# Gate and up of the feed-forward layers with the weights stationary, from the third slab on

## The chip, the cores and the metric

One core of a Trainium2 chip runs the whole program. The metric is the device time of one execution in microseconds, the median of three runs.

## The reference

The input is a sequence of 256 tokens of 1024 channels, float32. Four layers follow one another. Each has a token mixer (short convolution, pooling, differential attention, convolution) and a feed-forward layer, and each of the eight sub-layers stands between two norms. What the change touches is the feed-forward part:

```python
def _rms(x, g):
    y = xf * lax.rsqrt(jnp.mean(xf * xf, axis=-1, keepdims=True) + EPS)
    return (y * g.astype(jnp.float32)).astype(x.dtype)

def _swiglu(xn, w_gate, w_up, w_down):
    return (jax.nn.silu(xn @ w_gate) * (xn @ w_up)) @ w_down

        f = _swiglu(_rms(x, g[2]), ffn_w_gate[i], ffn_w_up[i], ffn_w_down[i])
        x = x + _rms(f, g[3])
```

The inner width of the feed-forward layer is 2816.

## The kernel before

**Precision.** Every matmul of a weight runs three times in the float32r format: a weight `raw` is split into `hi` (a cast on ScalarE, ACT) and `lo` (raw minus hi, on VectorE, DVE), an activation in the same way into `xh` and `xl` (or `hh` and `hl`, `zh` and `zl`), and hi with xh, lo with xh and hi with xl are added up in one PSUM bank.

**Tiling.** The 256 tokens are two tiles `t` of 128. The inner width is cut into NS = 11 slabs of 256 channels; a slab's weights are 256 columns of gate beside 256 columns of up. `proj` (line 263) makes one bank for one token tile and one slab: over eight pieces k of the 1024 input channels, xh or xl of the tile is the stationary operand (128x128) and 512 weight columns move, 24 matmuls. `evac` (475) takes the bank off: silu of the gate half with the token's rstd as scale on ACT, and on DVE the product with the up half and rstd, which gives `h`, tokens on the partitions. `flush` (483) turns h around with two transposes on TensorE (PE) and splits the result into hh (ACT) and hl (DVE), channels on the partitions. `down` (277) then has 128 columns of hh or hl stationary and 512 columns of the down weights moving, 12 matmuls for each token tile and slab, into four banks `acc` that stay open over the whole layer.

**Stages of a layer.** `start` (413) makes slabs 0 and 1 of token tile 0 while the norm before is still at work on tile 1. Then tile 1 of slabs 0 and 1 follows (513), and from slab 2 on (519) each turn of the loop makes both token tiles of slab s and then the down blocks of slab s-2 for both. The h of a bank is transposed after the next bank (`flush(1)`). `finish` (427) has the down blocks of the last three slabs, first all of tile 0 and then all of tile 1, with the norm (`boundary`, 336) of tile 0 beside tile 1's.

**What sets the order.** Every instruction is pinned to the program's order on its engine. `Weights` prepares the weights ahead: `pump(k)` (148) casts and subtracts up to k halves of a weight tile where fewer than NP = 12 halves are ahead of their release, and a subtraction that frees a raw tile lets the next load go on SP's queue. The places of the pump calls are therefore the places of this work in the queues of ACT and DVE. `boundary` squares and sums the sub-layer's output on ACT, multiplies it by the gain and the constant RS_C on DVE (`post`), computes the reciprocal root in seven small DVE operations and adds the result to x.

**PSUM.** Four banks acc, two banks mm (taken in turn by proj), two banks tr (transposes).

Of the kernel before, what the change touches and what calls it, by code (L numbers as in the profile page):

```python
# [9 lines left out]
F32 = mybir.dt.float32  # L10
# [143 lines left out]
class Kernel:  # L154
    def __init__(self, ctx, tc, x, w, gains, taps, pscale, lam, subg, rel, onehot, band, gcol, out):
        self.tc, self.nc = tc, tc.nc
        nc = self.nc
        self.V, self.A, self.T = Pinned(tc, nc.vector), Pinned(tc, nc.scalar), Pinned(tc, nc.tensor)
        self.G, self.SP = Pinned(tc, nc.gpsimd), Pinned(tc, nc.sync)
        self.w, self.gains, self.taps, self.out = w, gains, taps, out  # L160
        self.pscale, self.lamv, self.subg, self.rel = pscale, lam, subg, rel
        self.onehot, self.band = onehot, band
        pool = lambda name, bufs=1, **k: ctx.enter_context(tc.tile_pool(name=name, bufs=bufs, **k))
        self.c = pool("c")
        self.wraw = pool("wraw", NR)
        self.wsp = pool("wsp", NP)
        self.gp = pool("gp", 1)
        self.st = pool("st", 12)
        ps = bass.MemoryType.PSUM
        self.ps_acc = pool("ps_acc", 4, space=ps)  # L170
        self.ps_mm = pool("ps_mm", 2, space=ps)
        self.ps_tr = pool("ps_tr", 2, space=ps)
        self.dram = pool("dram", 1, space=bass.MemoryType.DRAM)
        self.wi = 0
        self.W = Weights(self, w.shape[0])
        self.x = self.c.tile([P, 2, D], F32, name="x")
        xv = x.rearrange("(t p) d -> p t d", p=P)
        self.gc = self.c.tile([P, 2, 8], F32, name="gc")
        self.A.dma_start(out=self.gc, in_=gcol)
        self.gc, self.gcp = self.gc[:, 0, :], self.gc[:, 1, :]  # L180
        xload = lambda t, h: self.SP.dma_start(
            out=self.x[:, t, h * 512 : (h + 1) * 512], in_=xv[:, t, h * 512 : (h + 1) * 512]
        )
        xload(0, 0)
        self.W.load()
        xload(1, 0)
        xload(0, 1)
        self.W.load()
        xload(1, 1)
        self.ident = self.c.tile([P, P], F32, name="ident")  # L190
        make_identity(nc, self.ident)
        self.xh = [self.c.tile([P, 8, P], F32R, name=f"xh{t}") for t in range(2)]
        self.xl = [self.c.tile([P, 8, P], F32R, name=f"xl{t}") for t in range(2)]
        self.r2 = [self.c.tile([P, 1], F32, name=f"rstd{t}") for t in range(2)]
        self.xg, self.s2 = [None, None], [None, None]

# [66 lines left out]
    def proj(self, t, slab, bank, k0=0, k1=8):  # L263

        T = self.T
        for k in range(k0, k1):
# [7 lines left out]
            if k % 2:  # L274
                self.W.used(i, c)

    def down(self, t, wid, zh, zl, accs, first, last, n_outer=False):

        T = self.T
        order = []  # L280
        for c in range(2):
            hi, lo = self.W.get(wid, c)
            order += [(c, zh, hi, 0), (c, zh, hi, 1), (c, zh, lo, 0), (c, zh, lo, 1), (c, zl, hi, 0), (c, zl, hi, 1)]
        if n_outer:
            order.sort(key=lambda o: o[3])
        left = [6, 6]
        for c, z, wt, n in order:
            left[n] -= 1
            T.matmul(
                accs[n],  # L290
                z[c],
                wt[:, n * 512 : (n + 1) * 512],
                start=first and left[n] == 5,
                stop=last and left[n] == 0,
            )
        for c in range(2):
            self.W.used(wid, c)
# [35 lines left out]
        else:  # L333
            self.A.activation(self.junk(), x, AF.Square, scale=1.0 / 32, accum_out=o)

    def boundary(self, t, m, g_post, g_pre, nxt, rstd=None, fill=()):


        V, A, W = self.V, self.A, self.W
        fill = [*fill, 0, 0, 0, 0]  # L340
        s = self.stat()
        mg = self.gp.tile([P, D], F32, tag="mg", name="mg")
# [1 line left out]
        H = [slice(0, 512), slice(512, 1024)]  # L344

        def post(h):
            V.scalar_tensor_tensor(mg[:, H[h]], m[h], RS_C, g_post[:, H[h]], op0=ALU.mult, op1=ALU.mult)

        def add(sl):
            V.scalar_tensor_tensor(x[:, sl], mg[:, sl], y, x[:, sl], op0=ALU.mult, op1=ALU.add)  # L350
# [3 lines left out]
                V.tensor_tensor(mg[:, H[h]], x[:, H[h]], g_pre[:, H[h]], op=ALU.mult)  # L354

        for h in range(2):
            A.activation(self.junk(), m[h], AF.Square, scale=1.0 / 32, accum_out=s[:, h : h + 1])
        W.sub(fill[0])
        post(0)
        W.sub(fill[1])  # L360
# [63 lines left out]
        self.x_rstd(1)  # L424


    def finish(self, outs, g_post, g_pre, nxt, zs):


        W = self.W  # L430
# [12 lines left out]
                W.pump(2)  # L443
        if nxt == "pool":
            tile(1, 0)
            self.boundary(0, accs[0], g_post, g_pre, nxt, None, (0, 0, 1, 1))
            for i in range(1, n):
                tile(1, i)
            self.boundary(1, accs[1], g_post, g_pre, nxt, None, (0, 0, 1, 1))
            return  # L450
        self.boundary(0, accs[0], g_post, g_pre, nxt)
        for i in range(n):
            if i == 2 and nxt == "x":
                self.x_transposed(0)
# [2 lines left out]
                self.x_transposed(0)  # L457
            if i == n - 3 and nxt == "x":
                W.pump(2)
        self.boundary(1, accs[1], g_post, g_pre, nxt, 0 if nxt == "x" else None)  # L460

    def ffn(self, pool, g_post, g_pre, nxt, tables=None):
        V, A, W = self.V, self.A, self.W
# [11 lines left out]
        def evac(t, s, bank):  # L475
            sg = pool.tile([P, 256], F32, tag="sg", name="sg", bufs=2)
            A.activation(sg, bank[:, 0:256], AF.Silu, scale=self.r2[t])
            h = pool.tile([P, 256], F32, tag="h", name="h", bufs=2)
            V.scalar_tensor_tensor(h, bank[:, 256:512], self.r2[t], sg, op0=ALU.mult, op1=ALU.mult)
            hs[t, s] = h  # L480
            pend.append((t, s))

        def flush(keep=0):
            while len(pend) > keep:
                t, s = pend.pop(0)
                if s not in hT:
                    hT[s] = (
                        pool.tile([P, 2, S], F32R, tag="hh", name="hh", bufs=4),
                        pool.tile([P, 2, S], F32R, tag="hl", name="hl", bufs=4),
                    )  # L490
                h, b = hs.pop((t, s)), self.tr()
                self.transposes(b, [h[:, 0:P], h[:, P : 2 * P]])
                sl = slice(t * P, (t + 1) * P)
                self.split(
                    b[:, 0:256].rearrange("p (c n) -> p c n", c=2), hT[s][0][:, :, sl], hT[s][1][:, :, sl]
                )
# [13 lines left out]
        if tables:  # L510
            next(tables, None)
        accs = [[self.acc(), self.acc()] for _ in range(2)]
        for s in range(2):
            b = self.mm()
            self.proj(1, slabs[s], b)
            evac(1, s, b)
            flush(1)
            self.pump()
        for s in range(2, NS):
            for t in range(2):  # L520
                b = self.mm()
                self.proj(t, slabs[s], b)
                evac(t, s, b)
                flush(1)
                self.pump()
            if tables:
                next(tables, None)
            if s < NS - 1:
# [4 lines left out]
        zs = []  # L533
        for s in range(NS - 3, NS):
            zh, zl = zpair(s)
            zs.append((dw[s], zh, zl, False, flush if s == NS - 2 else None))

        self.finish(accs, g_post, g_pre, nxt, zs)

    def conv(self, pool, layer, g_post, g_pre, nxt, cold=False):  # L540
        V, A, W = self.V, self.A, self.W
# [532 lines left out]
```

## Time and profile before

| | us |
|---|---|
| median of three runs | 1100.31 (1099.93 to 1101.47) |
| the profiled execution, its own time | 1100.8 |
| its span, first to last instruction | 1098.8 |

The page of the profile gives busy times of each engine, the span in 40 slices, the chain of work that ended last and the costliest groups of instructions. PE is the row of matmuls and PEld the row of weight loads, which run beside them. A matmul's duration contains its latency, and successive matmuls overlap, so what one costs in a stream is read from the distance between starts and not from its duration. In the names of a group the tile that is written stands ahead of the arrow, the moving and the stationary operand behind it.

### The profile page before, as it was taken

What the parts mean: (1) busy time and instruction counts of PE and PEld (TensorE: products, weight loads), DVE (VectorE), ACT (ScalarE), POOL (GpSimd) and SP (SyncE); (2) the same over time, 40 slices, a digit from 0 to 9 for tenths busy, and PEclk for the clock granted to TensorE, in tenths of its full rate; (3) what the DMA queues carried; (4) which work ended last, traced back from release to release, by engine and by line L of the source; (5) the groups of instructions that cost most, each with busy time, mean ns of one, the idle gap of its engine ahead of it and who ended that gap; (6) DMA issues with size and microseconds to landing.
All of it is one profiled execution on the core that took longest, in us unless ns stands there. A gap on an engine that the chain in (4) does not pass through costs nothing.

```text
span 1098.8 us, 12977 instructions
## 1 busy us (share of the span) xinstructions
PE 1085.5 (99%) x4990; PEld 885.8 (81%) x4990; DVE 696.2 (63%) x1171; ACT 529.9 (48%) x855; POOL 18.9 (2%) x40
## 2 busy tenths in 40 slices
PE   8999999999999999999999999999999999999997
PEld 6887888888888878888888788888888878888885
DVE  7877764555888464556786874545578677645543
ACT  6555553443556344445575563444445455534421
POOL 0000000000010001000000000000000000000000
PEclk9999999999999999999999999999999999999999
DMA  7864565545336556543544465545536544555421
GB/s 269 283 233 173 211 223 215 194 154 191 146 140 243 196 189 244 192 164 143 199 147 154 153 235 196 208 165 191 175 136 237 189 183 171 214 197 203 154 77 39
DMA packets 31486, 203.98 MB, mean 186 GB/s; under 512 B 3820, under 2 KB 4364, under 8 KB 8512
## 3 DMA queue, kind: packets, MB, share of 16 engines
q1 hardware_dynamic: 27648, 191.38, 47.7%
q0 software_dynamic: 3344, 11.24, 3.0%
q8 instruction: 39, 0.64, 0.2%
q10 hardware_dynamic: 432, 0.53, 0.1%
q14 instruction: 23, 0.19, 0.0%
HBM read 202.08 MB, written 2.11 MB: 186 GB/s over the span
## 4 chain that ended last, share of the span: by engine, by line
PE 94%; DVE 4%; ACT 1%; DMA 1%; issue 1%; SPq 0%; DVEq 0%; ACTq 0%
PE mm L48 62%; PE acc L48 28%; PE tr L48 4%; DVE st L48 1%; DVE lo L48 1%; DVE x L48 1%; DMA x<-in_x 1%; DVE mg L48 1%; ACT junk L48 0%; ACT xh L48 0%; DVE xl L48 0%; ACT hi L48 0%; SPq L48 0%; DVE ol L48 0%; DVE rstd L48 0%
## 5 line engine op out<-in xcount | busy, mean ns | idle before, releaser
L48 DVE TENSOR_TENSOR lo<-raw,hi 128x1024 fp32r<-128x1024 f32 (+1 forms) x374 | 426.1, 1187 | 57.7 <-ACT hi L48 56.8
L48 PE MATMUL mm<-hi,xh 128*128 128x512 f32 x976 | 390.8, 400 | 1.1 <-ACT hi L48 0.9
L48 PE MATMUL mm<-hi,xl 128*128 128x512 f32 x976 | 383.6, 393 | 0.2
L48 PE MATMUL mm<-lo,xh 128*128 128x512 f32 x976 | 382.6, 392 | 0.2 <-DVE lo L48 0.2
L48 ACT CAST hi<-raw 128x1024 fp32r<-128x1024 f32 (+1 forms) x374 | 361.6, 1028 | 12.9 <-DMA raw<-in_w 5.3
L48 PEld LDWEIGHTS mm<-hi,xl 128*128 128x128 f32 x976 | 183.3, 188 | 42.6 <-DVE xl L48 2.7
L48 PEld LDWEIGHTS mm<-hi,xh 128*128 128x128 f32 x976 | 183.5, 188 | 38.5 <-ACT hi L48 1.1
L48 PEld LDWEIGHTS mm<-lo,xh 128*128 128x128 f32 x976 | 183.7, 188 | 38.1 <-DVE lo L48 0.5
L48 ACT ACTIVATE sg<-mm,rstd 128x256 f32<-128x256 f32 x88 | 41.8, 475 | 356.6 <-PE mm L48 356.4
L48 DVE SCALAR_TENSOR_TENSOR h<-mm,rstd,sg 128x256 f32<-128x256 f32 x88 | 42.6, 484 | 263.7 <-ACT sg L48 263.7
L48 PE MATMUL acc<-hi,hh 128*128 128x512 f32 x352 | 116.9, 406 | 0.0
L48 PE MATMUL acc<-hi,hl 128*128 128x512 f32 x352 | 113.2, 395 | 0.0
L48 PE MATMUL acc<-lo,hh 128*128 128x512 f32 x352 | 112.7, 394 | 0.0
L48 PEld LDWEIGHTS acc<-lo,hh 128*128 128x128 f32 x352 | 66.2, 188 | 15.8
L48 PEld LDWEIGHTS acc<-hi,hl 128*128 128x128 f32 x352 | 66.2, 188 | 15.5
L48 PEld LDWEIGHTS acc<-hi,hh 128*128 128x128 f32 x352 | 63.3, 189 | 13.0 <-issue 0.9
L48 ACT ACTIVATE junk<-x 128x512 bf16<-128x512 f32 x30 | 18.9, 632 | 50.7 <-DVE x L48 50.7
L48 DVE TENSOR_TENSOR hl<-tr,hh 128x256 fp32r<-128x256 f32 x88 | 36.5, 415 | 2.3 <-ACT hh L48 2.3
L48 ACT ACTIVATE junk<-acc 128x512 bf16<-128x512 f32 x32 | 19.1, 598 | 32.9 <-PE acc L48 32.4
L48 PEld LDWEIGHTS tr<-ident,h 128*128 128x128 f32 x176 | 24.5, 139 | 11.7
L48 PE MATMUL tr<-ident,h 128*128 128x128 f32 x176 | 33.5, 272 | 0.0
L48 ACT CAST hh<-tr 128x256 fp32r<-128x256 f32 x88 | 32.2, 366 | 2.5 <-PE tr L48 2.5
(147 smaller groups left out, 666.7 us busy)
## 6 DMA issues: line engine op xcount, KB each, us to landing
raw<-in_w SPq DMA_DIRECT2D x179, 1024.0 KB, 4.8
gpost<-in_gains POOLq DMA_DIRECT2D x8, 512.0 KB, 4.1
gpre<-in_gains POOLq DMA_DIRECT2D x6, 512.0 KB, 5.7
raw<-in_w SPq DMA_DIRECT2D x3, 512.0 KB, 7.4
x<-in_x SPq DMA_DIRECT2D x4, 256.0 KB, 6.5
bandf<-in_band POOLq DMA_DIRECT2D x4, 256.0 KB, 4.8
skew<-scr POOLq DMA_DIRECT2D x4, 256.0 KB, 5.9
bias<-skew POOLq DMA_DIRECT2D x4, 192.0 KB, 5.5
```

The lines of the kernel that those rows point to most:

```text
L48: r = f(*a, **k)
```

## The change

Slabs 0 and 1 stay as they are, but for the rstd factor of the up half. From slab 2 on, the weights are the stationary operand: `proj_t` takes 128 columns of gate and the same 128 of up (index j, two of them in a slab) and moves both token tiles at once, 256 columns, as two pieces of 128 that lie apart in the joined tiles xhs and xls. A bank holds gate in one half and up in the other, channels on the partitions and tokens along the row. It takes 48 matmuls of 256 columns, and a slab has two such banks, as before. `evac_t` multiplies the gate half by `rows` (rstd of each token along the row, the same on every partition) on DVE, applies silu on ACT, multiplies by the up half on DVE, and writes hh and hl directly; there is no h to be transposed. One weight preparation stands between hh and hl, two behind.

The rstd factor of the up half is left out in all slabs. Down is linear, so the whole output of a layer lacks a factor per token; `boundary` puts it back with per-token scales `cols` (rstd/32 for the squares, RS_C times rstd for `post`). `rows` is made once a layer by two transposes of a tile whose columns all hold rstd.

```diff
+        self.xhs, self.xls = (self.c.tile([P, 2, 8, P], F32R, name=f"x{n}") for n in "hl")
+        self.xh, self.xl = ([a[:, t] for t in range(2)] for a in (self.xhs, self.xls))
+        self.ones = self.c.tile([P, P], F32, name="ones")
+        self.G.memset(self.ones, 1.0)
...
+    def proj_t(self, j, slab, bank):
+        T = self.T
+        for k in range(8):
+            i, c = slab[k // 4], k % 4 // 2
+            hi, lo = self.W.get(i, c)
+            xh, xl = self.xhs[:, :, k, :], self.xls[:, :, k, :]
+            for q in range(2):
+                o = (k % 2) * 512 + q * 256 + j * P
+                sl = slice(o, o + P)
+                b = bank[:, q * S : (q + 1) * S].rearrange("p (t n) -> p t n", t=2)
+                T.matmul(b, hi[:, sl], xh, start=k + q == 0, stop=False)
+                T.matmul(b, hi[:, sl], xl, start=False, stop=False)
+                T.matmul(b, lo[:, sl], xh, start=False, stop=k + q == 8)
+            if k % 2:
+                self.W.used(i, c)
...
-    def boundary(self, t, m, g_post, g_pre, nxt, rstd=None, fill=()):
+    def boundary(self, t, m, g_post, g_pre, nxt, rstd=None, fill=(), scale=None):
+        s32, sc = scale or (1.0 / 32, RS_C)
...
-            V.scalar_tensor_tensor(mg[:, H[h]], m[h], RS_C, g_post[:, H[h]], op0=ALU.mult, op1=ALU.mult)
+            V.scalar_tensor_tensor(mg[:, H[h]], m[h], sc, g_post[:, H[h]], op0=ALU.mult, op1=ALU.mult)
...
-            A.activation(self.junk(), m[h], AF.Square, scale=1.0 / 32, accum_out=s[:, h : h + 1])
+            A.activation(self.junk(), m[h], AF.Square, scale=s32, accum_out=s[:, h : h + 1])
...
-            V.scalar_tensor_tensor(h, bank[:, 256:512], self.r2[t], sg, op0=ALU.mult, op1=ALU.mult)
+            V.tensor_tensor(h, bank[:, 256:512], sg, op=ALU.mult)
...
+        def evac_t(s, j, bank):
+            sg = pool.tile([P, S], F32, tag="sg", name="sg", bufs=2)
+            V.tensor_tensor(sg, bank[:, 0:S], rows, op=ALU.mult)
+            A.activation(sg, sg, AF.Silu)
+            h = pool.tile([P, S], F32, tag="h", name="h", bufs=2)
+            V.tensor_tensor(h, bank[:, S : 2 * S], sg, op=ALU.mult)
+            new(s)
+            hh, hl = (a[:, j, :] for a in hT[s])
+            A.copy(hh, h)
+            W.pump(1)
+            V.tensor_tensor(hl, h, hh.bitcast(F32), op=ALU.subtract)
...
+        for t in range(2):
+            V.tensor_scalar(cols[:, t, 0:1], self.r2[t], 1.0 / 32, None, op0=ALU.mult)
+            V.tensor_scalar(cols[:, t, 1:2], self.r2[t], RS_C, None, op0=ALU.mult)
+            A.activation(rb[:, t, :], self.ones, AF.Copy, scale=self.r2[t])
         for s in range(2):
             b = self.mm()
             self.proj(1, slabs[s], b)
             evac(1, s, b)
+            if s == 0:
+                b = self.tr()
+                self.transposes(b, [rb[:, t, :] for t in range(2)])
+                A.copy(rows, b[:, 0:S])
             flush(1)
             self.pump()
         for s in range(2, NS):
-            for t in range(2):
+            for j in range(2):
                 b = self.mm()
-                self.proj(t, slabs[s], b)
-                evac(t, s, b)
-                flush(1)
-                self.pump()
+                self.proj_t(j, slabs[s], b)
+                evac_t(s, j, b)
+                flush()
+                W.pump(2)
...
-            zs.append((dw[s], zh, zl, False, flush if s == NS - 2 else None))
+            zs.append((dw[s], zh, zl, False, None))
+        scales = [(cols[:, t, 0:1], cols[:, t, 1:2]) for t in range(2)]
```

## Rows read from the trace of the kernel before

**Rows 1.** The page: span, busy time and share of each engine, granted clock in tenths.

```profile
span 1098.8 us, 12977 instructions
PE 1085.5 (99%) x4990; PEld 885.8 (81%) x4990; DVE 696.2 (63%) x1171; ACT 529.9 (48%) x855; POOL 18.9 (2%) x40
PEclk9999999999999999999999999999999999999999
```

**Rows 2.** The page: the chain that ended last, by engine.

```profile
PE 94%; DVE 4%; ACT 1%; DMA 1%; issue 1%; SPq 0%; DVEq 0%; ACTq 0%
```

**Rows 3.** Waits of PE: us in total, times, longest us.

```profile
PE acc L48 <- DVE lo L48: 1.5, 1, 1.5
...
PE tr L48 <- DVE mg L48: 0.2, 1, 0.2
```

**Rows 4.** The chain in order of time, one slab: start, us, what.

```profile
157.28 5.58 PE acc L48 x24
162.86 5.50 PE mm L48 x24
168.36 0.22 PE tr L48 x2
168.58 5.51 PE mm L48 x24
...
174.31 5.58 PE acc L48 x24
```

**Rows 5.** Groups by line: count, busy us, mean ns, idle before.

```profile
L48 PE MATMUL tr<-ident,h 128*128 128x128 f32 x176 | 33.5, 272 | 0.0
L48 PEld LDWEIGHTS mm<-hi,xh 128*128 128x128 f32 x976 | 183.5, 188 | 38.5 <-ACT hi L48 1.1
```

**Rows 6.** PE's instructions in order of time, pool mixer: start us, duration us.

```profile
294.05 0.40 PE L48 MATMUL mm<-bandh,xh 128*128 128x256 f32 x2
...
295.93 0.40 PE L48 MATMUL tr<-bandh,xl 128*128 128x256 f32 x2
...
303.43 0.39 PE L48 MATMUL mm<-bandh,xl 128*128 128x256 f32 x2
...
304.79 0.39 PE L48 MATMUL tr<-bandh,xl 128*128 128x256 f32 x2
305.02 0.28 PE L48 MATMUL acc<-hi,ph 128*128 128x256 f32 x1
...
310.59 0.28 PE L48 MATMUL acc<-hi,pl 128*128 128x256 f32 x1
```

**Rows 7.** Busy us by stretch: us, PE, PEld, DVE, ACT, POOL, clock, DMA share, GB/s.

```profile
162.90:168.30 5.40, 5.40 (x25) 4.37 (x24) 2.29 (x3) 0.20 (x1) 0.54 (x1) 1.00 0.98 388
305.10:310.50 5.40, 5.40 (x48) 5.40 (x47) 4.73 (x14) 3.54 (x9) 0.00 (x0) 1.00 0.15 61
```

**Rows 8.** Groups by line: evacuation of a bank and weight preparation.

```profile
L48 DVE TENSOR_TENSOR lo<-raw,hi 128x1024 fp32r<-128x1024 f32 x350 | 410.5, 1221 | 57.0 <-ACT hi L48 56.1
L48 DVE SCALAR_TENSOR_TENSOR h<-mm,rstd,sg 128x256 f32<-128x256 f32 x88 | 42.6, 484 | 263.7 <-ACT sg L48 263.7
L48 DVE TENSOR_TENSOR hl<-tr,hh 128x256 fp32r<-128x256 f32 x88 | 36.5, 415 | 2.3 <-ACT hh L48 2.3
...
L48 ACT CAST hi<-raw 128x1024 fp32r<-128x1024 f32 x350 | 347.9, 1055 | 11.6 <-DMA raw<-in_w 4.7 <-issue 3.5 <-DVE raw L48 2.2
L48 ACT ACTIVATE sg<-mm,rstd 128x256 f32<-128x256 f32 x88 | 41.8, 475 | 356.6 <-PE mm L48 356.4
L48 ACT CAST hh<-tr 128x256 fp32r<-128x256 f32 x88 | 32.2, 366 | 2.5 <-PE tr L48 2.5
```

**Rows 9.** DVE in order of time, end of the third feed-forward layer.

```profile
791.22 4.63 DVE L48 TENSOR_TENSOR lo<-raw,hi 128x1024 fp32r<-128x1024 f32 x4 [0.39 <-ACT hi L48]
```

**Rows 10.** Groups by line: DVE, 512 wide, with a scalar operand and with a constant.

```profile
L48 DVE SCALAR_TENSOR_TENSOR x<-mg,st,x 128x512 f32<-128x512 f32 x30 | 22.5, 751 | 0.9
L48 DVE SCALAR_TENSOR_TENSOR mg<-acc,gpost 128x512 f32<-128x512 f32 x32 | 21.9, 685 | 16.2 <-ACT junk L48 16.2
```

More of the change, by code (lines that the diff above doesn't have):

```diff
@@ L191, in __init__ @@
         make_identity(nc, self.ident)
-        self.xh = [self.c.tile([P, 8, P], F32R, name=f"xh{t}") for t in range(2)]
-        self.xl = [self.c.tile([P, 8, P], F32R, name=f"xl{t}") for t in range(2)]
+        self.xhs, self.xls = (self.c.tile([P, 2, 8, P], F32R, name=f"x{n}") for n in "hl")
+        self.xh, self.xl = ([a[:, t] for t in range(2)] for a in (self.xhs, self.xls))
+        self.ones = self.c.tile([P, P], F32, name="ones")
+        self.G.memset(self.ones, 1.0)
         self.r2 = [self.c.tile([P, 1], F32, name=f"rstd{t}") for t in range(2)]
@@ L424, in start, with finish @@
         self.x_rstd(1)
-    def finish(self, outs, g_post, g_pre, nxt, zs):
+    def finish(self, outs, g_post, g_pre, nxt, zs, scales=(None, None)):
         W = self.W
@@ L445, in finish @@
             tile(1, 0)
-            self.boundary(0, accs[0], g_post, g_pre, nxt, None, (0, 0, 1, 1))
+            self.boundary(0, accs[0], g_post, g_pre, nxt, None, (0, 0, 1, 1), scales[0])
             for i in range(1, n):
                 tile(1, i)
-            self.boundary(1, accs[1], g_post, g_pre, nxt, None, (0, 0, 1, 1))
+            self.boundary(1, accs[1], g_post, g_pre, nxt, None, (0, 0, 1, 1), scales[1])
             return
-        self.boundary(0, accs[0], g_post, g_pre, nxt)
+        self.boundary(0, accs[0], g_post, g_pre, nxt, scale=scales[0])
         for i in range(n):
@@ L459, in finish @@
                 W.pump(2)
-        self.boundary(1, accs[1], g_post, g_pre, nxt, 0 if nxt == "x" else None)
+        self.boundary(1, accs[1], g_post, g_pre, nxt, 0 if nxt == "x" else None, scale=scales[1])
     def ffn(self, pool, g_post, g_pre, nxt, tables=None):
@@ L478, in evac, with new @@
             h = pool.tile([P, 256], F32, tag="h", name="h", bufs=2)
-            V.scalar_tensor_tensor(h, bank[:, 256:512], self.r2[t], sg, op0=ALU.mult, op1=ALU.mult)
+            V.tensor_tensor(h, bank[:, 256:512], sg, op=ALU.mult)
             hs[t, s] = h
             pend.append((t, s))
+        def new(s):
+            if s not in hT:
+                hT[s] = (
+                    pool.tile([P, 2, S], F32R, tag="hh", name="hh", bufs=4),
+                    pool.tile([P, 2, S], F32R, tag="hl", name="hl", bufs=4),
+                )
+        def evac_t(s, j, bank):
[9 more added lines that the diff above has]
+            V.tensor_tensor(hl, h, hh.bitcast(F32), op=ALU.subtract)
         def flush(keep=0):
@@ L485, in flush @@
                 t, s = pend.pop(0)
[L486 to L490, printed above, removed]
+                new(s)
                 h, b = hs.pop((t, s)), self.tr()
@@ L512, in ffn @@
         accs = [[self.acc(), self.acc()] for _ in range(2)]
+        rows, cols = pool.tile([P, S], F32, name="rows"), pool.tile([P, 2, 2], F32, name="cols")
+        rb = pool.tile([P, 2, P], F32, name="rb")
+        for t in range(2):
+            V.tensor_scalar(cols[:, t, 0:1], self.r2[t], 1.0 / 32, None, op0=ALU.mult)
+            V.tensor_scalar(cols[:, t, 1:2], self.r2[t], RS_C, None, op0=ALU.mult)
+            A.activation(rb[:, t, :], self.ones, AF.Copy, scale=self.r2[t])
         for s in range(2):
@@ L535, in ffn @@
             zh, zl = zpair(s)
[L536 to L538 removed]
+            zs.append((dw[s], zh, zl, False, None))
+        scales = [(cols[:, t, 0:1], cols[:, t, 1:2]) for t in range(2)]
+        self.finish(accs, g_post, g_pre, nxt, zs, scales)
     def conv(self, pool, layer, g_post, g_pre, nxt, cold=False):
```

## The prediction

> **What bounds the kernel now.** I read the page from the top. The busy line [rows 1] shows TensorE (PE) busy for 1085.5 of 1098.8 us, and the clock row stands at 9 in every slice, so the clock is at its upper level throughout and the change has no cold stretch to save. The chain of work that ended last lies 94% on PE [rows 2], and the seven waits that PE has in the whole run, from 1.5 down to 0.2 us each, add up to 4.7 us [rows 3]. So whatever leaves PE's instruction stream leaves the time, and whatever enters it is paid in full. VectorE (DVE) and ScalarE (ACT) are busy for 63% and 48% [rows 1].
>
> The chain in order of time [rows 4] gives one slab of a feed-forward layer: 24 matmuls of token tile 0, two transposes, 24 matmuls of token tile 1, two transposes, 24 matmuls of the down projection. That is 5.50 + 0.22 + 5.51 + 0.22 + 5.58 = 17.03 us, and the next slab begins exactly there (174.31 - 157.28), so there is no gap in it. One matmul of 128x512 thus steps on in 5.50/24 = 229.2 ns in gate and up, and in 5.58/24 = 232.5 ns in down. One transpose is 0.11 us.
>
> **The change, part by part.**
>
> *Transposes removed.* Slabs 2 to 10 of four layers are 36 slabs, each with two pairs of transposes on the chain: 36 x 0.44 = 15.8 us. The trace has 176 of them [rows 5]; 144 go, 32 stay (slabs 0 and 1). Nothing hides them today: PE goes from the last matmul of a bank to the transposes and back.
>
> *Matmuls reshaped.* The columns that are streamed stay the same, 24 x 512 per bank then and 48 x 256 now, but there are twice as many matmuls. Each one loads its stationary operand even when it equals the one before: the counts of matmuls and of loads are the same, 4990 [rows 1], although gate and up use xh twice in a row. So the loads double as well, and everything hangs on the step of a 256-wide matmul, c. A slab's gate and up cost 5.50 + 5.51 + 0.44 = 11.45 us before, and 96 c after; break-even of this part is c = 119.3 ns.
>
> The trace shows 256-wide matmuls of the same type in the pool mixer alone [rows 6]. Three stretches give three steps. The second stage there runs 48 in a row, hi and lo moving, from 305.02 to 310.59: 47 steps of 118.5 ns. The band stage of token tile 0 goes from 294.05 to 295.93 with 16 steps, 117.5 ns. That of token tile 1 goes from 303.43 to 304.79 with 12 steps, 113.3 ns. The first of these is the nearest in length and in its accumulating on one region of a bank several times in a row, but its operands differ. The other anchor is the same operands at twice the width: half of 229.2 ns is 114.6 ns, and this is what c would be if a step were columns alone. I take c = 117 ns, in between and nearer to the longer stretches, and keep 113.3 and 118.5 as the ends that rows show. No row has a moving operand in two pieces, which the new one is (128 columns of either token tile, 4 KB apart); that could add something, and I see no reason for it to gain. So the cost of a slab goes from 11.45 to 96 x 0.117 = 11.23 us, a gain of 0.22 us, and over 36 slabs 7.9 us.
>
> At 256 columns the weight-load row of PE is full: 5.40 of 5.40 us with 256-wide matmuls, 4.37 of 5.40 with 512-wide ones [rows 7]. One load starts with every matmul in either. By the Trainium skill (TensorE: Matmul & The Clock Gate, Back-to-back issue gap) the spacing of a stream is set by the load and the matmul together, and narrow matmuls pay for it: about 81 ns at 128 columns where the columns alone give 56. An estimate by the Trainium skill's figures there, the same 25 ns for every load on top of the 109 ns that it gives for 256 columns, makes 134 ns here and a time near 1152 us; the 48 steps of 118.5 ns do not bear that out. Against it stands the Trainium skill (same title, Step-by-step: what each phase is for, step 1): loading the next weights takes no read bandwidth from the running matmul. By that one c is the half of the wide step; the stretch of 118.5 speaks against it, that of 113.3 for it. Both come back as rivals.
>
> *Added on PE:* two transposes a layer, of the rstd rows: 8 x 0.11 = 0.9 us. They stand after the first bank of token tile 1, 5.5 us after rb was asked for, so PE does not wait for them.
>
> *The evacuation.* Before, ACT (silu, 475 ns) and DVE (product, 484 ns) read the bank, then PE, ACT (366) and DVE (415) made hh and hl [rows 8]. After, DVE multiplies by the rows (nearest row: 415), ACT does silu (475), DVE the product (415), ACT hh (366), DVE hl (415). DVE thus gets 3 x 415 - 484 - 415 = 0.35 us more per bank, 0.7 us per slab of 16.8; it is busy for 63%, so this is cover and no cost. The bank is free about 1.5 us after its last matmul, and PE needs that buffer again only after the other bank of the pair, 5.6 us or more later. The down projection of a slab runs two iterations later, so it does not wait either. If that cover were gone, the 1.4 us of product and silu would show once per bank.
>
> *The moved pump.* One weight preparation (a cast of 1055 ns on ACT, a subtraction of 1221 on DVE) now stands between hh and hl, and hl is queued behind it. Someone waits for hl soon only at the end of a layer: the last slab's second half feeds the third down block. From the bank's end: 415 + 475 + 415 + 366 + 1055 + 1221 + 415 = 4.4 us, and with 0.05 us at each hand-over some 4.7. The first two down blocks cover 24 x 232.5 ns = 5.6 us, and the third, ordered by output half, reads that hl with its sixth matmul, at 6.7 us. I count nothing. In the layer read for this, four such subtractions stood in a row on DVE at that point, 4.63 us [rows 9]; if two of them came ahead of hl in place of one, hl would be 1.2 us later, still before 6.7. SP's weight loads keep their order; POOL gets one small memset, behind the identity that PE waits for at the start and ahead of nothing that is due then.
>
> *Up's scale in the norm.* The product on DVE loses its scalar operand; the post-norm product gets one in place of a constant. A 512-wide operation with such an operand takes 751 ns, one with a constant 685 [rows 10]: 66 ns, twice per boundary. Where PE's next work covers a boundary it costs nothing; it lies open at the end of the program and ahead of the pool mixer, where nothing follows that could cover it. Some 0.2 us, an estimate of three such pieces. The squares and the four small products for cols cost nothing that shows: they run while a bank of 5.5 us is filled.
>
> *Sum:* -7.9 + 0.9 + 0.2 = -6.8 us. The profiled execution took 1100.8 us (span 1098.8 and 2.0 around it), 0.5 over the median of 1100.31. I subtract from the median: **1093.5 us**.
>
> **The rivals.**
>
> *The step is columns alone.* Then c is 113.3 to 114.6 ns, a slab costs 10.88 to 11.00 us, the gain is 0.57 to 0.45 us a slab, 20.6 to 16.2 in all, and with the 1.1 us added the time is 1080.8 to 1085.2. For it: the band stretch of token tile 1, and the steady 229.2 of the same operands. Against it: the longest stretch.
>
> *The loads eat the gain.* With c = 118.5 a slab costs 11.38, the gain is 2.7 us, less 1.1 added: 1098.7, no change that can be told. For it: the longest and steadiest stretch. Against it: its operands lie elsewhere, and two of three stretches are below.
>
> *The two-piece moving operand costs (slower).* Two matmuls of 118.5 take 237.0 where one of 229.2 carries the same columns: a break between two matmuls costs 7.8 ns. If a break inside the operand costs the same, c = 126.3, a slab 12.12 us, 0.67 more than now, 24.3 in all, and the time is 1125.7. It decides the sign from c = 119.0 on (96 c = 11.45 less 1.1/36). For it: no row shows that such an operand is free. Against it: none shows that it is not.
>
> *The load sets the step (slower).* A load lasts 188 ns in its own row [rows 5]; at 512 columns a step of 229 covers it, at 256 it does not. If a matmul had to wait for the whole of it, c = 188, a slab 18.05 us, 6.6 more, and the time 1100.3 + 237.6 + 1.1 = 1339. The 256-wide stretches contradict it: they step on in 118.5 ns so there the loads overlap one another. It is the rule of the Trainium skill's Back-to-back issue gap, taken to its extreme.
>
> *It does not do what it says.* If PE were not the bound, the transposes would cost nothing now; rows 2 to 4 exclude that.
>
> **How the numbers follow.** About 0.2%, 2.2 us, is what a measurement of this kernel can tell from no change. Chances: forecast (c from 115 to 118) 0.42; columns alone 0.20; loads eat the gain (118 to 119.6) 0.18; two pieces 0.18; load 0.02. Faster by over 0.2% are the first two and the edge of the third, 0.63; the rest of the third is 0.17; slower are the last two, 0.20. The range goes from 1080 (the cheapest row) to 1106, where c is 120.8 and a third of the two-piece price is in; the dearer part of that case and the load stay out, some 0.15.
>
> **What would show it.** The chain between two down blocks of a layer should be 2 x 5.62 us of matmuls and no transposes; the first matmul to last of one bank gives c directly. A layer's slab should take 16.8 us in place of 17.03. PE should not wait for DVE or ACT at the third down block. The forecast is wrong if c is outside 115 to 118, if PE shows waits inside the slabs, or if the down blocks leave their 5.58 us.

## The result and the profile after

| | us |
|---|---|
| before, median in the same comparison | 1100.46 |
| after, median (1085.00 to 1087.04) | 1085.76 |
| ratio, 95% interval | 0.9865 (0.9853 to 0.9877) |
| profiled execution of after, its own time / its span | 1087.04 / 1085.3 |

The change takes 14.7 us off, 13.5 to 16.2 by the interval. The forecast was 6.8. The sign was right and the time lies in the range, but the gain is more than twice as large as the sum said.

The page of after, to be laid beside [rows 1]: the span, then busy time and count of each engine.

```profile
span 1085.3 us, 16404 instructions
PE 1069.7 (99%) x6582; PEld 943.9 (87%) x6582; DVE 723.5 (67%) x1259; ACT 541.5 (50%) x867; POOL 19.1 (2%) x41
```

PE is still the bound at 99%. It executes 1592 instructions more: 36 slabs x 48 more matmuls are 1728, 144 transposes fewer and 8 more make 1592. DVE has 27.3 us more work; 0.35 us for 72 banks would be 25.

The chain in order of time, between two down blocks of the first feed-forward layer (start, us, what), beside [rows 4]:

```profile
148.50 10.89 PE mm L48 x96
159.38 5.58 PE acc L48 x24
164.96 10.89 PE mm L48 x96
175.85 5.58 PE acc L48 x24
```

This is the main reading. Between two down blocks there are matmuls and nothing else, and 96 of them take 10.89 us: **c = 113.4 ns**, where the forecast had 117. A slab takes 16.47 us in place of 17.03. Down keeps its 5.58.

One bank in each layer differs: the first of the new kind. The chain where it begins:

```profile
131.36 0.22 PE tr L48 x2
131.58 5.66 PE mm L48 x48
137.24 0.22 PE tr L48 x2
```

Here 48 matmuls take 5.66 us, 117.9 ns each. The later banks of the four layers run at 113.3 to 113.8, and in three of the four layers a slab from the next one on takes the 10.89 us above, in the second 10.91. The granted clock is 1.00, the upper of its two levels (1.2 and 2.4 GHz), in both kinds of bank (us, PE, PEld, DVE, ACT, POOL, clock, DMA share, GB/s):

```profile
131.30:137.00 5.70, 5.70 (x51) 5.70 (x50) 4.25 (x5) 3.58 (x5) 0.00 (x0) 1.00 0.83 306
148.40:153.80 5.40, 5.40 (x50) 5.40 (x49) 4.68 (x5) 2.35 (x3) 0.00 (x0) 1.00 0.61 209
```

The waits of PE (us in total, times, longest), beside [rows 3]:

```profile
PE acc L48 <- DVE lo L48: 1.5, 1, 1.5
PE tr L48 <- ACT rb L48: 1.4, 4, 0.4
...
PE tr L48 <- DVE mg L48: 0.2, 1, 0.2
```

The second line is new: in each of four layers PE waits 0.4 us for rb. No wait inside the slabs and none at the third down block has appeared, so the evacuation and the moved pump are hidden, as the prediction had it. All instructions around the first of these waits, in order of time (start, us, engine, operation, idle before and what ended it):

```profile
120.86 2.36 DVE L48 TENSOR_TENSOR lo<-raw,hi 128x1024 fp32r<-128x1024 f32 x2 [0.46 <-ACT hi L48]
...
123.57 1.06 DVE L48 SCALAR_TENSOR_TENSOR st<-st 128x1 f32<-128x1 f32 x5
...
124.66 0.15 DVE L48 TENSOR_SCALAR rstd<-st 128x1 f32<-128x1 f32 x1
124.67 0.27 PE L48 MATMUL tr<-ident,rb 128*128 128x128 f32 x1
...
124.85 0.40 ACT L48 ACTIVATE rb<-ones,rstd 128x128 f32<-128x128 f32 x1 [2.77 <-DVE rstd L48]
...
125.30 0.33 PE L48 MATMUL tr<-ident,rb 128*128 128x128 f32 x1 [0.36 <-ACT rb L48]
```

rb of token tile 1 needs rstd of that tile. On DVE two weight subtractions, 2.36 us together, and the seven small operations of the reciprocal root stand ahead of it, so rstd is there at 124.81 and rb at 125.25. PE had transposed tile 0's rb at 124.67 and stood idle for 0.36 us.

The groups of the new evacuation, by line (count, busy us, mean ns, idle before), beside [rows 8]:

```profile
L48 DVE TENSOR_TENSOR h<-mm,sg 128x256 f32<-128x256 f32 x88 | 37.4, 424 | 56.0 <-ACT sg L48 56.0
L48 DVE TENSOR_TENSOR sg<-mm,rows 128x256 f32<-128x256 f32 x72 | 30.5, 424 | 96.6 <-PE mm L48 96.6
L48 ACT ACTIVATE sg<-sg 128x256 f32<-128x256 f32 x72 | 30.1, 418 | 271.3 <-DVE sg L48 271.3
L48 DVE TENSOR_TENSOR hl<-h,hh 128x256 fp32r<-128x256 f32 x72 | 30.1, 418 | 0.9 <-ACT hh L48 0.9
```

Estimated were 415 ns for each DVE step and 475 for silu; 418 to 424 and 418 came.

### The profile page after: what moved, and what is told of

Its sections match the earlier page's. It is cut to its first block, busy times and chain, and to the rows that moved or that the text cites. A ratio compares the mean times of both kernels' runs of the same rounds, so it can differ in the third digit from the quotient of the medians.

```text
span 1085.3 us, 16404 instructions
## 1 busy us (share of the span) xinstructions
PE 1069.7 (99%) x6582; PEld 943.9 (87%) x6582; DVE 723.5 (67%) x1259; ACT 541.5 (50%) x867; POOL 19.1 (2%) x41
## 4 chain that ended last, share of the span: by engine, by line
PE 87%; DVE 7%; ACT 3%; issue 2%; DMA 1%; SPq 0%; DVEq 0%; ACTq 0%
PE mm L48 59%; PE acc L48 26%; DVE lo L48 3%; PE tr L48 2%; DVE st L48 2%; ACT hi L48 1%; DVE x L48 1%; DVE mg L48 1%; DMA raw<-in_w 1%; ACT junk L48 0%; DVE xl L48 0%; ACT xh L48 0%; ACT sg L48 0%; ACT rb L48 0%; DVE raw L48 0%
## 5 line engine op out<-in xcount | busy, mean ns | idle before, releaser
L48 PE MATMUL mm<-xh,hi 128*128 128x256 f32 x1152 | 319.2, 277 | 0.0
L48 PE MATMUL mm<-xl,hi 128*128 128x256 f32 x1152 | 318.4, 276 | 0.0
L48 PE MATMUL mm<-xh,lo 128*128 128x256 f32 x1152 | 318.4, 276 | 0.0
L48 PEld LDWEIGHTS mm<-xh,hi 128*128 128x128 f32 x1152 | 216.4, 188 | 1.4
L48 PEld LDWEIGHTS mm<-xl,hi 128*128 128x128 f32 x1152 | 216.3, 188 | 1.5
L48 PEld LDWEIGHTS mm<-xh,lo 128*128 128x128 f32 x1152 | 216.4, 188 | 0.0
L48 PE MATMUL mm<-hi,xh 128*128 128x512 f32 x400 | 163.0, 407 | 1.2 <-ACT hi L48 1.0
L48 PE MATMUL mm<-hi,xl 128*128 128x512 f32 x400 | 157.9, 395 | 0.3
L48 PE MATMUL mm<-lo,xh 128*128 128x512 f32 x400 | 157.0, 393 | 0.4 <-DVE lo L48 0.4
L48 PE MATMUL acc<-hi,hh 128*128 128x512 f32 x352 | 113.5, 396 | 0.0
L48 PEld LDWEIGHTS mm<-lo,xh 128*128 128x128 f32 x400 | 75.6, 189 | 15.7 <-DVE lo L48 1.1
L48 PEld LDWEIGHTS acc<-hi,hl 128*128 128x128 f32 x352 | 66.1, 188 | 15.3
```

The lines of the kernel that those rows point to most:

```text
L48: r = f(*a, **k)
```

## The experiments

**What was open.** First theory: a narrow step is columns alone, and the pool mixer's 118.5 belongs to something in its own operands or surroundings. Its rivals: 113.4 is what weights-stationary order gives and weights-moving does not; or it hangs on where the operands lie in a partition of SBUF. Beside that, the small terms (rb, norm, transposes, pump) were each to be measured alone. A step is the mean distance between the ends of successive matmuls, of one block of 24 or 48, or of all blocks of one form (the operands named) in a kernel; where 96, 48 or 24 are shown, the row of the chain divided by their number gives the same within 0.3 ns.

### Which half of the change matters

`before_halves`: the kernel before, each 512-wide matmul of gate and up from slab 2 on cut in two.

```diff
+            for q in range(2):
+                o = (k % 2) * 512 + q * 256
+                sl = slice(o, o + 256)
+                b = bank[:, q * 256 : (q + 1) * 256]
+                T.matmul(b, xh, hi[:, sl], start=k + q == 0, stop=False)
+                T.matmul(b, xh, lo[:, sl], start=False, stop=False)
+                T.matmul(b, xl, hi[:, sl], start=False, stop=k + q == 8)
```

> The kernel before, with one edit: in the feed-forward slabs 2 to 10 each matmul of 512 weight columns is cut into two of 256 (x stays stationary, transposes and evacuation as before). 3456 narrow matmuls in place of 1728. Theory A (columns alone: the step of a narrow matmul is half of the wide one whatever moves): step near 113.4 to 114.6 ns, time 1096 to 1100. Theory B (it is the weights being stationary that makes the step cheap; with weights moving it is the 118.5 ns of the pool mixer): a bank takes 5.69 us in place of 5.51, time near 1113.

Measured 1111.56 us, ratio 1.0102 (1.0087 to 1.0117). The chain of this kernel:

```profile
152.56 5.66 PE mm L48 x48
158.22 0.22 PE tr L48 x2
158.43 5.58 PE acc L48 x24
```

5.66/48 = 117.9 ns: narrow matmuls with the weights moving cost 11 us by themselves. So 256 wide is not 113.4 as such, and "columns alone" does not hold in general.

`down_quarters`: after, with down's matmuls cut in 256 columns too (four weight quarters in place of two halves in `down`).

> The changed kernel with every down projection (feed-forward, conv, attention) cut from 512 to 256 moving weight columns. Theory A: a block of two tiles takes 48 x 113.4 = 5.44 us in place of 5.58, 56 blocks, time near 1078. Theory B (weights moving, 118.5 ns): 5.69 us, time near 1092.

Measured 1091.71 us, 0.9920 (0.9904 to 0.9937). Down's narrow matmuls step on in 118.6 ns, 119.9 in the second feed-forward layer; those of the convolution (zh) in 116.7; those of attention (oh) in 117.7 to 117.9, but for one block of 48 at 113.5. One kernel thus holds steps from 113.4 to 119.9 for the same shape.

`idle_transposes`: after, with two transposes of the identity put back behind each new bank; nothing reads them.

```diff
                 flush()
+                self.transposes(self.tr(), [self.ident, self.ident])
                 W.pump(2)
```

> The changed kernel with two transposes of the identity, which nothing reads, put back behind each of the 72 narrow banks. If the transposes lay on the path in full: 72 x 0.22 = 15.8 us more than 1085.8, 1101.6. If their removal was worth less because something else now ends last: less than that.

Measured 1103.81 us, 1.0027 (1.0017 to 1.0038): 18.0 us over after. The chain:

```profile
164.05 5.46 PE mm L48 x48
169.50 0.22 PE tr L48 x2
169.72 5.47 PE mm L48 x48
```

The transposes themselves are 72 x 0.22 = 15.8 us, the prediction's term to the digit. The rest is a narrow step of 113.9 instead of 113.4 in most banks and 117.9 in seven of the 72, where after has four. Without the transposes' removal the change would have lost time.

### What sets 113.4 or 118

`one_piece`: the moving operand lies in one piece of 256 columns.

```diff
-        self.xhs, self.xls = (self.c.tile([P, 2, 8, P], F32R, name=f"x{n}") for n in "hl")
+        self.xhs, self.xls = (self.c.tile([P, 8, 2, P], F32R, name=f"x{n}") for n in "hl")
...
-            xh, xl = self.xhs[:, :, k, :], self.xls[:, :, k, :]
+            xh, xl = (a[:, k].rearrange("p t n -> p (t n)") for a in (self.xhs, self.xls))
```

> The changed kernel with xh and xl laid out so that the 256 moving columns of a k lie in one piece. If pieces are free: step 113.4 ns as now, time within 1 us of 1085.8. If the break in the moving operand costs part of what the step has over half a 512-wide transposing stream (109 ns): step down to 109 to 112 ns, time 1071 to 1081.

Measured 1085.44 us, 0.9863 (0.9848 to 0.9877); 96 matmuls in 10.89 us again. Two pieces cost nothing: that rival falls.

`order_hlh`: hi with xh, lo with xh, hi with xl, so that the stationary operand changes at each matmul.

```diff
                 T.matmul(b, hi[:, sl], xh, start=k + q == 0, stop=False)
-                T.matmul(b, hi[:, sl], xl, start=False, stop=False)
-                T.matmul(b, lo[:, sl], xh, start=False, stop=k + q == 8)
+                T.matmul(b, lo[:, sl], xh, start=False, stop=False)
+                T.matmul(b, hi[:, sl], xl, start=False, stop=k + q == 8)
```

> The changed kernel with the three products of a piece in the order hi xh, lo xh, hi xl in place of hi xh, hi xl, lo xh, so that no stationary operand comes twice in a row and the moving one does. If the order does not matter: step 113.4, 1085.8. If a repeated stationary operand is what makes the step cheap: near 118 ns, 1101.

Measured 1086.31 us, 0.9868 (0.9849 to 0.9888), 10.89 us for 96: the order of the products is indifferent.

`x_elsewhere`: xhs and xls come from a pool allocated behind the weights.

```diff
+        self.xp = pool("xp")
...
-        self.xhs, self.xls = (self.c.tile([P, 2, 8, P], F32R, name=f"x{n}") for n in "hl")
+        self.xhs, self.xls = (self.xp.tile([P, 2, 8, P], F32R, name=f"x{n}") for n in "hl")
```

> The changed kernel with xh and xl allocated behind the weight tiles in SBUF, no other edit. If the cheap step of 113.4 ns comes from the role (x moves, the weights stand): 113.4 as now, 1085.8. If it comes from where the moving operand lies: the step goes to about 118 ns and the time to near 1101.

Measured 1105.83 us, 1.0045 (1.0029 to 1.0061). Same instructions, and 20 us more than after:

```profile
164.09 11.51 PE mm L48 x96
```

11.51/96 = 119.9 ns. So the place of the operands counts. The program's allocation gives each tile's start address in a partition: in after, xh is at 192 and the weights at 256 modulo 512 bytes, moving minus stationary -64; in x_elsewhere both are at 256. This made a second theory: the distance between the two start addresses sets the step. Its rival was the place itself (ahead of or behind the weights, or one operand's own alignment). Five kernels moved tiles in SBUF and changed nothing else. The first diff is shift64, with 64 bytes of padding ahead of x and 64 behind it; both64 has the one ahead alone. elsewhere64 has the same two in the pool of x_elsewhere, elsewhere192 one of 48 elements there (second diff), and elsewhere448 the pool st and the small tile gc, both between the weights and x (third diff).

```diff
+        self.c.tile([P, 16], F32, name="pada")
         self.xhs, self.xls = (self.c.tile([P, 2, 8, P], F32R, name=f"x{n}") for n in "hl")
+        self.c.tile([P, 16], F32, name="padb")
```

```diff
+        self.xp.tile([P, 48], F32, name="pada")
         self.xhs, self.xls = (self.xp.tile([P, 2, 8, P], F32R, name=f"x{n}") for n in "hl")
```

```diff
+        self.st = pool("st", 12)
+        self.xp = pool("xp")
         self.gp = pool("gp", 1)
-        self.st = pool("st", 12)
...
-        self.gc = self.c.tile([P, 2, 8], F32, name="gc")
+        self.gc = self.xp.tile([P, 2, 8], F32, name="gc")
```

> The changed kernel with 64 bytes of padding ahead of xh and xl and 64 behind them: they move by 64 bytes, the weight tiles by 128. Their start goes from 64 to 0 modulo 128, that of the weight tiles stays 0; the place ahead of the weights stays. Theory P (place in SBUF: the moving operand has to lie ahead of the weights): step 113.4 ns, 1085.8. Theory A (alignment: both operands on the same offset modulo 128 bytes is what costs): step near 119.9 ns as in the kernel with x behind the weights, 1105.8.

> The changed kernel with 64 bytes of padding ahead of xh and xl and none behind: xh and xl start at 0 modulo 128, the weight tiles at 64. If it is the difference of the two operands' offsets that counts: step 113.4 ns, near 1086. If it is which of them has the offset 64 (x standing with 64 and weights moving with 0 gave 117.9 ns in the kernel before with halves): step 117.9 ns, near 1101.

> The kernel with xh and xl behind the weights, and 64 bytes of padding ahead of them, so that their start is 64 modulo 128 as in the changed kernel. Theory P: step 119.9 ns, 1105.8. Theory A: step 113.4 ns, 1085.8.

Measured: shift64 1107.80 us, 1.0063 (1.0045 to 1.0081); both64 1084.85, 0.9854 (0.9836 to 0.9872); elsewhere64 1100.63, 1.0001 (0.9991 to 1.0011). The chain of shift64:

```profile
165.13 11.52 PE mm L48 x96
```

and of elsewhere64:

```profile
164.60 11.31 PE mm L48 x96
175.91 5.48 PE acc L48 x24
```

Padding ahead and behind costs 22 us, the same padding ahead alone, which moves x and weights together, costs nothing. It is not either operand's own address. In elsewhere64 the narrow step is 117.8 and down got faster (5.48 us) as its distance went from 128 to 0.

> xh and xl behind the weights again, now placed so that the start of the moving operand is 64 bytes below that of the stationary one modulo 512, as in the changed kernel (with 64 above it the step was 117.8 ns, with none 119.9). Theory D (the distance of the two starts modulo 512 is all that counts, place and role do not): step 113.4 ns for the narrow matmuls, 1083 to 1086. Theory P (x behind the weights costs of itself): 117.8 ns, near 1100.

> The same with the moving operand 192 bytes above the stationary one modulo 512. If the distance counts modulo 256 (192 is then 64 below): 113.4 ns, 1085 to 1087. If modulo 512: another step, 117 to 120 ns, 1099 to 1107.

Measured: elsewhere448 1088.05 us, 0.9885 (0.9865 to 0.9905); elsewhere192 1092.96, 0.9930 (0.9910 to 0.9950). Both lie behind the weights, at distances of -64 and +192, and both have the cheap step back for most or half of their matmuls: the place ahead of the weights falls as a cause. But the distance does not settle it either. The chain of elsewhere192 in the third feed-forward layer:

```profile
655.86 10.90 PE mm L48 x96
666.76 5.59 PE acc L48 x24
672.35 11.31 PE mm L48 x96
683.66 5.60 PE acc L48 x24
689.26 10.90 PE mm L48 x96
```

One slab runs at 113.5 ns, the next at 117.8, and so on, in three of its layers; in the other one all eight slabs after the first run at 113.6. In elsewhere448 three layers are cheap and the second is not. Neither the clock nor the work beside PE tells a cheap slab of elsewhere192 from a dear one (us, PE, PEld, DVE, ACT, POOL, clock, DMA share, GB/s):

```profile
689.30:700.10 10.80, 10.80 (x97) 10.80 (x96) 5.73 (x7) 2.77 (x5) 0.00 (x0) 1.00 0.60 206
705.80:717.00 11.20, 11.20 (x97) 11.20 (x96) 5.72 (x7) 2.76 (x5) 0.00 (x0) 1.00 0.59 200
```

### Putting it to use

`rows_later`: after, with the transposes of rb one bank later (behind the flush of the second bank).

```diff
-            if s == 0:
-                b = self.tr()
-                self.transposes(b, [rb[:, t, :] for t in range(2)])
-                A.copy(rows, b[:, 0:S])
             flush(1)
             self.pump()
+            if s == 1:
+                b = self.tr()
+                self.transposes(b, [rb[:, t, :] for t in range(2)])
+                A.copy(rows, b[:, 0:S])
```

> The changed kernel with the two transposes of the rstd rows put behind the second bank of token tile 1 in place of the first. If the wait of TensorE for rb (0.36 us in each layer) is a real loss: 1.4 us less, 1084.3. If it only moves to the next thing that waits for rstd: no change, 1085.8.

Measured 1084.10 us, 0.9851 (0.9837 to 0.9866), 1.7 us under after, though the two intervals overlap. The wait for rb is gone from PE's list, which begins like this and has no line for it:

```profile
PE acc L48 <- DVE lo L48: 1.5, 1, 1.5
PE mm L48 <- POOL ident masks.py:199: 1.4, 1, 1.4
PE mm L48 <- ACT xh L48: 0.7, 2, 0.5
```

`one_piece_rows_later`, both edits together:

> Both edits that did not cost: moving operand in one piece and the rstd rows transposed after the second bank. The first bank of a layer ran at 117.9 ns a step in the changed kernel and at 113.8 in the one-piece one: if that is due to the layout, 4 x 0.2 us less than the 1084.1 of the later rows, 1083.3; if not, 1084.1.

Measured 1083.49 us, 0.9843 (0.9828 to 0.9857): not to be told from rows_later.

`align_down` is rows_later with padding that puts the weights 64 above hh (before: 128, in the second layer 96) and 64 below zh. `aligned` puts hh, zh and oh at distance 0, with 32 (24 in the second layer) and 8 in place of 16, 8 and 24 elements in the diff, which is align_down's, and with 16 more ahead of oh; 48 ahead of ph put the pool mixer's weights 64 below ph. The tiles allocated behind the padding (in a feed-forward layer also sg, h, rows and rb) move too.

```diff
+        pool.tile([P, 8 if tables_at == 3 else 16], F32, name="pad")
         hs, hT, pend = {}, {}, []
...
+        pool.tile([P, 24], F32, name="pad")
         zh = [pool.tile([P, 4, S], F32R, name=f"zh{j}")
...
```

> The later-rows kernel with padding that puts hh, hl, zh and zl, the stationary operands of the down projections, at 64 modulo 128 in place of 0, 32 and 96; the moving weights stay at 0. Theory A: a matmul of down steps on in 229.4 ns, as with oh in attention, which lies at 64, in place of 232.4 to 233.3: 33 feed-forward blocks x 24 x 3.0 ns, 11 x 24 x 3.8 and 8 conv blocks x 24 x 3.9 are 4.1 us, 1080.0. Theory P: no change, 1084.1.

> The later-rows kernel with padding alone: hh, hl, zh, zl, oh and ol start at the same place modulo 512 as the moving weights (512-wide matmuls stepped on in 228.2 to 228.7 ns where both started alike, 229.2 with the weights 64 above, 232.4 with 128, 233.2 with 32, 96 or 64 below), ph and pl 64 above the weights. Theory D: feed-forward down blocks at 228.2 in place of 232.4 and 233.2, conv's at 228.3 in place of 233.3: 3.3 + 1.3 + 1.0 us, and 0.3 for attention and the pool mixer, 1078.2. If it is not the distance: 1084.1.

Measured: align_down 1082.25 us, 0.9830 (0.9817 to 0.9844), the lowest median of all, with an interval that overlaps that of one_piece_rows_later; aligned 1090.54, 0.9907 (0.9892 to 0.9922). The chain of align_down:

```profile
667.60 10.91 PE mm L48 x96
678.51 5.49 PE acc L48 x24
```

and of aligned:

```profile
162.90 11.31 PE mm L48 x96
174.21 5.44 PE acc L48 x24
```

Down does what its distance says, 5.49 and 5.44 in place of 5.58. zh in align_down stayed at 233.4, so its padding bought nothing: it lay at -64 and hh at +64, so the two are not the same, and the expectation's reckoning modulo 128 does not hold. In aligned, 3312 of 3456 narrow matmuls ran at 117.8 although x and the weights stood at the very distance of after; in align_down 672 did. That the distance alone sets the narrow step is thereby refuted.

What else does is not shown. Down blocks in between are not all of it: in the second layer of aligned the second bank is dear already, ahead of the layer's first down block, where rows_later takes 5.46 us:

```profile
343.25 5.65 PE mm L48 x48
348.91 5.44 PE acc L48 x24
```

And in the second layer of align_down the level changes in the middle of the layer, with every tile where it was. A matmul of another form (32x512, for a table of the attention; the chain has it as tr, in two records) stands between two slabs there. The slab before it takes 10.91 us, the next and all later ones of the layer 11.31:

```profile
384.57 10.91 PE mm L48 x96
395.48 0.95 PE tr L48 x2
396.43 5.70 PE acc L48 x24
402.13 11.31 PE mm L48 x96
```

In before_halves the bank behind the same matmul and its down block is the only one of 72 at 113.4, and in shift64 the slab behind them goes from 120.0 to 118.6, for that slab alone; in rows_later the level stays. So the level looks like a state that lasts from slab to slab and that something passing can switch; no run separates what switches it.

### The small terms

`hl_first`: the pump between hh and hl goes behind hl.

```diff
             A.copy(hh, h)
-            W.pump(1)
             V.tensor_tensor(hl, h, hh.bitcast(F32), op=ALU.subtract)
+            W.pump(1)
```

> The changed kernel with the weight preparation put back behind hl. If nobody waits for hl, as reckoned: no change, 1085.8. If hl comes late for the third down block at the end of a layer: some tenths of a microsecond less.

Measured 1086.18 us, 0.9866 (0.9850 to 0.9883): no difference to after. The moved pump costs nothing.

`scale_only`: the kernel before with up's scale in the norm and nothing else (`scale` in boundary and finish, `cols`, a product without r2 in evac).

> Before, with only up's scale put into the norm: slabs from the third on still make one bank per token tile with the weights moving and still transpose h. As the prediction counts this term: three open boundaries at two operations each, 66 ns dearer, 0.2 us in a part of the program that nothing covers: 1100.7 us against 1100.5 of before, so no change that can be told; the 512-wide step stays 229.2 ns. If the norm's cost was under-counted and is part of the missing microseconds, the time is 1101.5 or more, and the distance from the last down block to the next first matmul is longer by the same amount at each layer's end.

Measured 1102.22 us, 1.0010 (1.0001 to 1.0019). Its groups by line, beside [rows 10]:

```profile
L48 DVE SCALAR_TENSOR_TENSOR mg<-acc,cols,gpost 128x512 f32<-128x512 f32 x16 | 11.9, 747 | 11.9 <-ACT junk L48 11.9
L48 ACT ACTIVATE junk<-acc,cols 128x512 bf16<-128x512 f32 x16 | 11.0, 687 | 21.6 <-PE acc L48 21.2 <-ACT junk L48 0.3
L48 DVE SCALAR_TENSOR_TENSOR mg<-acc,gpost 128x512 f32<-128x512 f32 x16 | 11.0, 685 | 4.6 <-ACT junk L48 4.6
L48 ACT ACTIVATE junk<-acc 128x512 bf16<-128x512 f32 x16 | 9.6, 599 | 10.6 <-PE acc L48 10.3
```

The product on DVE is 62 ns dearer, as predicted (66). The squares on ACT are 88 ns dearer (687 to 599), which the prediction had at nothing. Between the last down block before the pool mixer and the first matmul after it, this kernel loses 0.39 us against before, at the end of the program 0.16, and in between 0.26, where PE now waits at two more places:

```profile
PE tr L48 <- DVE mg L48: 0.6, 3, 0.2
```

Together 0.8 us, where the forecast had 0.2. Of the remaining 0.9 of the two spans' difference (1100.5 to 1098.8), 0.75 lies in the opening, ahead of the first norm with a scale, where the two programs are equal; after and rows_later, whose openings are equal too, differ there by 1.1 us.

## Why the prediction was right or wrong

**The bound: right.** What left PE's stream left the time, and what entered it was paid. The two transposes put back cost 15.8 us of their own, as computed.

**The step c: the failed step.** "I take c = 117 ns, in between and nearer to the longer stretches." It is 113.4, outside the 115 to 118 that the forecast gave itself. The term was -7.9; with 113.4 it is 36 x (11.45 - 10.89) = -20.2. The rival "columns alone" had the number (113.3 to 114.6) at a chance of 0.20, but not for its reason: before_halves has the same columns at 117.9 and shift64 at 120.0, so its number came true by the place at which the operands happened to lie. What misled is "the first of these is the nearest in length": the pool mixer's 118.5 was taken for the price of a narrow matmul, but there moving and stationary operand start 128 bytes apart, modulo 256, and in gate and up 64. In elsewhere192, whose distance in that stage of the pool is -64, the very same 48 matmuls step on in 113.6 (in aligned, at -64 too, in 117.9). [rows 6] had nearly shown both levels at the distance of the new gate and up: the moving band tiles start at -64 from xh and xl, and the same form stepped on in 117.5 for one token tile and in 113.3 for the other. The prediction set c between them, where no bank of gate and up ran in after. The better anchor was the steady 229.2 of the same operands: half of it is 114.6. But it was no sure one: before_halves, the same operands halved, gave 117.9.

**The loads** overlap in the step: a load lasts 188 ns in its own row of after, and one starts every 113.4. By the Trainium skill's figures (TensorE: Matmul & The Clock Gate, Back-to-back issue gap) the estimate was 134 ns; 113.4 with a load for every matmul does not bear it out. The same page's statement that loading takes no read bandwidth (Step-by-step: what each phase is for, step 1) agrees with 113.4, half of 229.2 within 1.2 ns, and does not say why 64 bytes of padding on either side of x make it 118.6 to 120.0.

**Two-piece operand: rightly kept out of the sum.** one_piece shows no cost.

**"PE does not wait for them": wrong,** though small. "5.5 us after rb was asked for" counted from rb's place in ACT's queue and not from its input: rstd of tile 1 was queued behind two subtractions on DVE. A layer pays 0.8 us for the rows: 0.22 for the transposes, 0.36 of wait, and the rest for the matmuls after it getting under way. That is 3.2 us where 0.9 was counted; rows_later gets 1.7 back.

**The norm: mis-sized,** 0.8 in place of 0.2. "The squares and the four small products for cols cost nothing that shows" overlooked that the squares too got a scale per token: 88 ns more on ACT. By the Trainium skill (ScalarE: Activation LUTs, What ACT_TABLE_LOAD costs) each operand of an activation that is given per partition adds about 93 ns over a constant; the trace agrees within 5 ns, and the rule would have supplied the missing price.

**Evacuation and moved pump: right.** No wait of PE on either; hl_first is the same as after.

**The sum with what was measured:** -20.2 for the step, +0.9 for four first banks at 117.9 (4 x 48 x 4.5 ns), +3.2 for the rows, +0.8 for the norm, -15.3 in all; -14.7 was measured, -16.2 to -13.5 by the interval.

**The range:** its upper end of 1106 goes with c = 120.6 and not 120.8; nothing hangs on it.

**What stays open.** Why a bank runs at 113.4 or 117.8 at one and the same distance. The first bank of a layer is at 117.9 in after and the rest is not; padding that left x and the weights at their distance and moved other tiles put nearly all narrow matmuls to 117.8; in align_down the level changes within a layer; in elsewhere192 it alternates from slab to slab, at the same clock and the same work of the other engines. There a slab uses 6 of the 12 buffers that the weights have, so two slabs in turn read different buffers; whether that is the reason was not tried.

## What to carry to other kernels

Price a new matmul shape by the step of the same operands in the trace (half of the wide step for half of the columns) before that of another stage with the same shape, and carry 6% of that step as uncertainty (113.4 to 119.9 here), because the operands' places in SBUF alone move it by that much. When a change adds an operation that PE reads, follow its input back through the queue of the engine that makes it, not only the operation's own place. After such a change, look at the step of each matmul group; a few bytes of padding can be worth more than the edit.

## What the runs showed of the hardware

In these kernels the step of a matmul stream went with the distance of the start addresses of its moving and its stationary operand in a partition, though not with it alone (moving minus stationary, float32r, 128 rows, one load for each matmul). The distance is taken modulo 256 bytes; elsewhere192, at +192, has the two levels of -64. Ordered over before, after and all experiments, the steps at 512 columns as the mean of all blocks of one form in a kernel (pauses over 0.3 us left out), those at 256 columns for each block of 48:

| distance | step at 512 columns, ns | step at 256 columns, ns |
|---|---|---|
| 0 | 226.8 to 228.4 | 119.7 to 120.0 |
| +64 | 229.0 to 229.9 | 117.7 to 117.9, three blocks 113.4 to 113.5 |
| 128 | 232.2 to 233.1 | 118.5 to 118.8 or 119.9 to 120.1 |
| -64 | 233.1 to 233.4 | 113.3 to 113.9 or 117.8 to 117.9 |
| +32 | 233.1 to 233.4 | 116.4 to 117.0 |
| +96 | 233.2 to 233.5 | 119.4 to 120.1 |
| -32 | 233.1 to 233.5 | not run |
| -96 | 233.9 to 234.2 | not run |

The order at 256 columns is not that at 512: distance 0 is the best for wide matmuls and among the worst for narrow ones. At 256 columns and -64 two levels exist, 4% apart, and a run of 96 matmuls stays in one. Through 36 slabs the difference between the placements of after and of shift64, the same program but for padding, is 22 us of 1086, more than the whole change gave. The table is an ordering of what was seen; its mechanism was not found.
